# The factor of the attention scores put into the queries, and the maximum taken negated

## The chip, the cores and the metric

The kernel runs on one core of a Trainium2 chip. The metric is the device time of one execution in microseconds (us), smaller is better; a kernel's time is the median of its runs. The engines of the core work side by side, each on its own queue of instructions in a fixed order: TensorE (PE in the rows; its weight loads stand apart as PEld), VectorE (DVE), ScalarE (ACT), GpSimd (POOL), and SyncE (SP), which issues most DMAs.

## The reference

Three mixer layers run one after the other over 512 positions of width 2048: two of a first kind, which also carry 256 context positions, and one of a second kind. In a layer of the first kind the input is scaled and shifted, projected by `w_in`, and split into a short convolution, a differential attention, and a pooling part; their joined output goes through `w_out` and a layer norm. What the change touches is the differential attention. It has 8 heads, each with two maps of 64 query and key features and one value of width 128:

```python
def _diff_attn(qb, k_all, v_all, lam):
    s = jnp.einsum('bqhid,bkhid->bhiqk', qb.astype(jnp.float32) * ATTN_SCALE, k_all.astype(jnp.float32))
    p = jax.nn.softmax(s, axis=-1)
    a = p[:, :, 0] - lam * p[:, :, 1]
    return jnp.einsum('bhqk,bkhe->bqhe', a.astype(v_all.dtype), v_all)
```

`ATTN_SCALE` is 64 to the power of -0.5, 0.125. Latent queries look at 768 keys (256 of the context and 512 latent ones); in layer 0 the context's 256 queries look at the 256 context keys as well.

## The kernel before

All products are made in float32r parts: an operand is split into a high part (`hi`, a rounded copy by ScalarE) and a low part (`lo`, source minus high part, by GpSimd or VectorE), and a product is the sum of three matmuls (`mm3`, L163). A *unit* is 128 output features of the projection: 16 steps of 128 inputs, each with three matmuls over 512 latent positions and, where the context takes part, three over 256. Its weights come by DMA as raw tiles of 128x512; ScalarE copies them to `whi` (L156), GpSimd subtracts to `wlo` (L140).

`attention` (L450) runs over 8 heads, once in each of the first two layers. Per head it makes four units: queries, keys, values, gate. `evict_q` (L319) applies the rotation (L314 to L317; VectorE and GpSimd), and splits the 64 rows of each map into a high and a low half of one 128-row tile: the copies L326 and L327 on ScalarE, the subtractions L328 and L329 on VectorE (they stand under the helper's line, L140, as `Q<-qr,Q`). `evict_k` does the same with the keys, and a DMA copies the halves; `evict_v` copies the values out (L345, L346, tile `vT`), transposes and splits them.

`attend` (L361) goes over blocks of 256 queries, twice 128, and for each 128 over the two maps: matmuls give the scores in `ps_s`, of which there is one buffer (two PSUM banks); VectorE takes the maximum over a row (L384), and multiplies it by -0.125 (L386, `nb`); ScalarE takes the exponential of 0.125 times the score plus `nb`, with the row's sum (L393); VectorE takes the reciprocal of the sum (L395). After both maps it multiplies the second reciprocal by minus lambda (L398, 128x1), normalizes the first map (L400) and adds the second (L401). TensorE transposes the result (L408), which is split again (L412, L413), and multiplies it with the values (L418). A head has 6 blocks of 128 queries in layer 0 and 4 in layer 1, with two maps each: 8 x 12 + 8 x 8 = 160 passes through L384 to L395.

During attention a second job runs along (`along`, `advance`, 3 or 4 steps per unit): products of a later layer's modulation weights with a vector, GpSimd multiplying (L805) and ScalarE summing (L806) through a single buffer, with a priority moved back by 800.

The order of instructions on each engine isn't the program's: `TileContext(nc, schedule_with_timeline_sim=True)` lays it out before the run from a timeline with costs of its own, by the instructions' dependences and priorities. On the chip each engine then keeps that order, and waits on semaphores.

Of the kernel before, what the change touches and what calls it, by code (L numbers as in the profile page):

```python
# [11 lines left out]
F32 = mybir.dt.float32  # L12
F32R = mybir.dt.float32r
BF16 = mybir.dt.bfloat16
AF = mybir.ActivationFunctionType
ALU = mybir.AluOpType
AX = mybir.AxisListType
# [29 lines left out]
def mixer_stack_kernel(ctx: ExitStack, tc: tile.TileContext, a: dict, out: bass.AP):  # L47
    nc = tc.nc
# [14 lines left out]
    def ps_s():  # L63
        return pp.tile([128, 2, 512], F32, name="ps_s", tag="s", bufs=1)

    def ps_t():
        return pp.tile([128, 512], F32, name="ps_t", tag="t", bufs=1)

    def ps_v():
        return pp.tile([128, 512], F32, name="ps_v", tag="v", bufs=1)  # L70
# [68 lines left out]
    def sub_lo(lo, src, hi, eng):  # L139
        eng.tensor_tensor(lo, src, hi.bitcast(F32), op=ALU.subtract)  # L140
# [171 lines left out]
    def rope(tp, dst, ps):  # L312
        sh = tp.tile([128, NL], F32, name="rsh", tag="rsh", bufs=1)
        nc.vector.stream_shuffle(sh, ps, SWAP16)  # L314
        nc.vector.tensor_tensor(dst, ps, rope_c, op=ALU.mult)
        nc.gpsimd.tensor_tensor(sh, sh, rope_s, op=ALU.mult)
        nc.gpsimd.tensor_tensor(dst, dst, sh, op=ALU.add)  # L317

    def evict_q(ap_, aq, u, T):  # L319
        qr = aq.tile([128, NT], F32, name="qr", tag="qr", bufs=1)  # L320
        rope(aq, qr[:, :NL], u.lat)
        if u.cx is not None:
            nc.scalar.copy(qr[:, NL:], u.cx)
        Q0 = ap_.tile([128, T], F32R, name="Q0", tag="Q0", bufs=2)
        Q1 = ap_.tile([128, T], F32R, name="Q1", tag="Q1", bufs=2)
        nc.scalar.copy(Q0[0:64, :T], qr[0:64, :T])  # L326
        nc.scalar.copy(Q1[64:128, :T], qr[64:128, :T])  # L327
        sub_lo(Q0[64:128, :T], qr[0:64, :T], Q0[0:64, :T], nc.vector)  # L328
        sub_lo(Q1[0:64, :T], qr[64:128, :T], Q1[64:128, :T], nc.vector)  # L329
        return Q0, Q1  # L330

    def evict_k(ap_, aq, u):
# [28 lines left out]
    def attend(ap_, l, h, Q, K, V, SG, T):  # L361
        Q0, Q1 = Q
        Vh, Vl = V
        for qp in range(T // 256):
            nkt = 6 if qp < 2 else 2
            nk = nkt * 128
            ncol = nk // 2 if nkt == 6 else nk
            nch = nk // ncol
            aTh = ap_.tile([128, 6, 256], F32R, name="aTh", tag="aTh", bufs=1)
            aTl = ap_.tile([128, 6, 256], F32R, name="aTl", tag="aTl", bufs=1)  # L370
            for qi in range(2):
                q0 = qp * 256 + qi * 128
                es, ds = [], []
                for m, (Qm, Km) in enumerate(((Q0, K[0]), (Q1, K[1]))):
                    ps = ps_s()
                    for c in range(nch):
                        o = ps[:, c, :ncol]
                        for i, kp in enumerate(Km):
                            nc.tensor.matmul(  # L379
                                o, Qm[:, q0:q0 + 128], kp[:, c * ncol:(c + 1) * ncol], start=i == 0, stop=i == 1  # L380
                            )
                    sv = ps[:, :nch, :ncol]
                    mx = ap_.tile([128, 1], F32, name="mx", tag="mx", bufs=4)
                    nc.vector.reduce_max(mx, sv, axis=AX.XY)  # L384
                    nb = ap_.tile([128, 1], F32, name="nb", tag="nb", bufs=4)
                    nc.vector.tensor_scalar(nb, mx, -0.125, None, op0=ALU.mult)  # L386
                    if m == 0:
                        e = ap_.tile([128, NT], F32, name="E0", tag="E0", bufs=2)
                        e = e[:, :nk].rearrange("p (c n) -> p c n", c=nch)
                    else:  # L390
                        e = sv
                    d = ap_.tile([128, 1], F32, name="dn", tag="dn", bufs=4)
                    nc.scalar.activation(e, sv, AF.Exp, bias=nb, scale=0.125, accum_out=d)  # L393
                    r = ap_.tile([128, 1], F32, name="rd", tag="rd", bufs=4)
                    nc.vector.reciprocal(r, d)  # L395
                    es.append(e)
                    ds.append(r)
                nc.vector.tensor_tensor(ds[1], ds[1], neglam[l], op=ALU.mult)  # L398
                E0, E1 = es
                nc.vector.tensor_scalar(E0, E0, ds[0], None, op0=ALU.mult)  # L400
                nc.vector.scalar_tensor_tensor(E0, E1, ds[1], E0, op0=ALU.mult, op1=ALU.add)  # L401
                kt_of = lambda kt: E0[:, kt * 128 // ncol, kt * 128 % ncol:kt * 128 % ncol + 128]
                for r in range((nkt + 2) // 3):
                    n = min(3, nkt - 3 * r)
                    tp = ps_t()
                    for i in range(n):
                        kt = 3 * r + i
                        nc.tensor.transpose(tp[:, i * 128:(i + 1) * 128], kt_of(kt), ident)  # L408
                    tv = tp[:, :n * 128].rearrange("p (k d) -> p k d", k=n)
                    dh = aTh[:, 3 * r:3 * r + n, qi * 128:(qi + 1) * 128]  # L410
                    dl = aTl[:, 3 * r:3 * r + n, qi * 128:(qi + 1) * 128]
                    nc.scalar.copy(dh, tv)  # L412
                    nc.vector.tensor_tensor(dl, tv, dh.bitcast(F32), op=ALU.subtract)  # L413
            ov = ps_v()
            o = ov[:, :256]
            for kt in range(nkt):
                for p, (v, t) in enumerate(((Vh, aTh), (Vh, aTl), (Vl, aTh))):
                    nc.tensor.matmul(  # L418
                        o, v[:, kt], t[:, kt], start=(kt == 0 and p == 0), stop=(kt == nkt - 1 and p == 2)
                    )  # L420
            y = SG[:, qp * 256:(qp + 1) * 256]
            nc.vector.scalar_tensor_tensor(y, o, subg[l], y, op0=ALU.mult, op1=ALU.mult)
            o2 = ap_.tile([128, 256], F32, name="o2", tag="o2", bufs=1)
            nc.scalar.square(o2, o)
            o2h = ap_.tile([128, 256], F32R, name="o2h", tag="o2h", bufs=1)
            o2l = ap_.tile([128, 256], F32R, name="o2l", tag="o2l", bufs=1)
            nc.scalar.copy(o2h, o2)
            sub_lo(o2l, o2, o2h, nc.vector)
            msv = ps_v()
            ms = msv[:, :256]  # L430
            nc.tensor.matmul(ms, ones_r, o2h, start=True, stop=False)
            nc.tensor.matmul(ms, ones_r, o2l, start=False, stop=True)
            if qp == 0:
                rt = ap_.tile([128, 512], F32, name="rt", tag="rt", bufs=1)
                nc.scalar.copy(rt[:, :256], ms)
                continue
            r = slice(256, 512) if qp == 1 else slice(0, 256)
            nc.scalar.copy(rt[:, r], ms)
            n = 512 if qp == 1 else 256
            nc.scalar.activation(rt[:, :n], rt[:, :n], AF.Sqrt, bias=eps_t, scale=8.0)  # L440
            for i in range(n // 256):
                q0 = (0, 256)[i] if qp == 1 else 512
                ri = rt[:, i * 256:(i + 1) * 256]
                y = SG[:, q0:q0 + 256]
                nc.vector.reciprocal(ri, ri)
                nc.vector.tensor_tensor(y, y, ri, op=ALU.mult)
            o = 0 if qp == 1 else 512
            nc.sync.dma_start(Yd[4 + h][:, o:o + n], SG[:, o:o + n])
# [849 lines left out]
```

## Time and profile before

| | |
|---|---|
| median of 3 runs | 3577.58 us (3574.09 to 3579.79) |
| the profiled execution's own time | 3577.58 us |
| its span, first to last instruction | 3575.8 us |
| mean granted TensorE clock | 0.959 of full speed |
| instructions | 48562 |

Busy time adds up each engine's instructions; weight loads run beside matmuls. The idle time before an instruction is put down to the one whose semaphore came last. [...] The chain that ended last is followed back from the last instruction, at each step to what released it or to the instruction before it on its engine.

### The profile page before, as it was taken

To read this page: it belongs to the slowest core of one execution; us is meant where nothing else is said; L and a number is where in the kernel's file an instruction comes from. 1 tells how busy PE (TensorE), PEld (TensorE's weight loads), DVE (VectorE), ACT (ScalarE), POOL (GpSimd) and SP (SyncE) were. 2 spreads that over 40 slices of the span, in tenths; PEclk is the share of its full clock that TensorE was granted. 3 is DMA by queue.
4 is the path that set the end of the run, shared out by engine and by line. 5 is a ranking of instruction groups with operands and counts; after the bars stand their busy time and mean duration, and the time that the engine had idled before them with its cause. 6 is when DMAs were issued, how large, how long until landed. Compare 5 with 4: busy or idle time off the path is not lost.

```text
span 3575.8 us, 48562 instructions
## 1 busy us (share of the span) xinstructions
PE 3301.2 (92%) x16850; PEld 2791.3 (78%) x16850; DVE 2324.2 (65%) x3649; ACT 1519.0 (42%) x3181; POOL 1958.8 (55%) x1436
## 2 busy tenths in 40 slices
PE   8898998989998899999999999998989899999997
PEld 7787887878886787778888888877668777777765
DVE  6845555555468538774565555585577899996576
ACT  2255666655431222243665654322445333345333
POOL 2356776765234543256877764587776444444432
PEclk8899999989998999999999999999999999999999
DMA  8744333333246447664554542586765222223565
GB/s 311 288 133 115 99 111 99 103 104 89 70 143 185 135 131 221 191 223 140 159 154 143 162 126 85 184 309 227 231 221 195 80 93 84 84 77 109 183 222 187
DMA packets 274150, 554.72 MB, mean 155 GB/s; under 512 B 30992, under 2 KB 40048, under 8 KB 265712
## 3 DMA queue, kind: packets, MB, share of 16 engines
q1 hardware_dynamic: 271344, 539.04, 46.9%
q0 software_dynamic: 2560, 12.58, 1.8%
q8 instruction: 132, 2.16, 0.3%
q14 instruction: 114, 0.93, 0.1%
HBM read 510.69 MB, written 28.23 MB: 151 GB/s over the span
## 4 chain that ended last, share of the span: by engine, by line
PE 49%; DVE 18%; DMA 12%; issue 8%; POOL 7%; ACT 6%; SPq 0%; DVEq 0%; POOLq 0%; ACTq 0%
PE ps_m L163 35%; DVE acc L989 5%; DMA wraw<-in_w_out_dram 5%; POOL wlo L140 3%; POOL gpr L805 3%; DVE gpr L809 2%; PE ps_m L232 2%; PE ps_s L379 2%; ACT whi L156 2%; DVE wlo L140 2%; PE ps_v L418 2%; DMA gw<-in_w_ada_dram 1%; PE ps_s L233 1%; PE ps_m L609 1%; DMA gv<-in_cc_dram 1%
## 5 line engine op out<-in xcount | busy, mean ns | idle before, releaser
L163 PE MATMUL ps_m<-h,whi 128*128 128x512 f32 (+1 forms) x4736 | 1611.2, 398 | 47.3 <-ACT vT L345 32.5
L140 POOL TENSOR_TENSOR wlo<-wraw,whi 128x512 fp32r<-128x512 f32 x768 | 1113.3, 1467 | 947.6 <-ACT whi L156 886.0
L163 PEld LDWEIGHTS ps_m<-h,whi 128*128 128x128 f32 x4736 | 899.9, 192 | 233.7 <-ACT vT L345 34.1
L156 ACT CAST whi<-wraw 128x512 fp32r<-128x512 f32 x1040 | 608.1, 618 | 881.1 <-DMA wraw<-in_w_out_dram 268.0
L163 PE MATMUL ps_m<-h,wlo 128*128 128x512 f32 (+1 forms) x2368 | 940.0, 397 | 0.1
L805 POOL TENSOR_TENSOR gpr<-gw,gv 128x512 f32<-128x512 f32 x320 | 425.8, 1331 | 240.9 <-ACT gpr L806 173.1
L163 PE MATMUL ps_m<-hc,whi 128*128 128x256 f32 x2048 | 554.5, 283 | 0.0
L163 PEld LDWEIGHTS ps_m<-h,wlo 128*128 128x128 f32 x2368 | 455.1, 192 | 93.8 <-POOL wlo L140 0.8
L163 PEld LDWEIGHTS ps_m<-hc,whi 128*128 128x128 f32 x2048 | 381.0, 190 | 3.4
L140 DVE TENSOR_TENSOR wlo<-wraw,whi 128x512 fp32r<-128x512 f32 x272 | 246.7, 921 | 202.3 <-ACT whi L156 201.7
L806 ACT ACTIVATE gpr<-gpr 128x512 f32<-128x512 f32 x320 | 201.8, 631 | 233.6 <-POOL gpr L805 232.9
L163 PE MATMUL ps_m<-hc,wlo 128*128 128x256 f32 x1024 | 288.9, 282 | 0.0
L989 DVE SCALAR_TENSOR_TENSOR acc<-gu,pack,acc 128x511 f32<-128x511 f32 (+24 forms) x240 | 232.7, 981 | 5.4
L609 PE MATMUL ps_m<-wlo,y 128*128 128x512 f32 x512 | 208.1, 407 | 21.2 <-POOL wlo L140 13.6
L809 DVE SCALAR_TENSOR_TENSOR gpr<-gw,gv 128x512 f32<-128x512 f32 x232 | 220.7, 951 | 8.4 <-DMA gw<-in_w_ada_dram 2.0
L610 PE MATMUL ps_m<-whi,y 128*128 128x512 f32 x512 | 204.2, 400 | 3.2 <-DVE y L140 3.2
L384 DVE TENSOR_REDUCE mx<-ps_s 128x1 f32<-128x768 f32 (+1 forms) x160 | 135.0, 844 | 102.0 <-PE ps_s L379 101.2
L163 PEld LDWEIGHTS ps_m<-hc,wlo 128*128 128x128 f32 x1024 | 194.9, 190 | 1.0
L608 PE MATMUL ps_m<-whi,y 128*128 128x512 f32 x512 | 183.3, 400 | 1.7 <-ACT y L582 0.8
L413 DVE TENSOR_TENSOR aTl<-ps_t,aTh 128x384 fp32r<-128x384 f32 (+1 forms) x144 | 77.4, 538 | 156.2 <-ACT aTh L412 156.0
L609 PEld LDWEIGHTS ps_m<-wlo,y 128*128 128x128 f32 x512 | 98.0, 191 | 56.5 <-POOL wlo L140 22.1
L379 PE MATMUL ps_s<-K,Q 128*128 128x384 f32 x576 | 133.3, 347 | 9.5 <-ACT E L393 5.2
(353 smaller groups left out, 5284.4 us busy)
## 6 DMA issues: line engine op xcount, KB each, us to landing
wraw<-in_w_in_dram SPq DMA_DIRECT2D x640, 256.0 KB, 2.9
wraw<-in_w_out_dram SPq DMA_DIRECT2D x384, 256.0 KB, 3.5
wm<-in_w_mod_dram SPq DMA_DIRECT2D x48, 1024.0 KB, 6.9
gw<-in_w_mod_dram SPq DMA_DIRECT2D x192, 256.0 KB, 3.4
gw<-in_w_ada_dram SPq DMA_DIRECT2D x136, 256.0 KB, 3.2
wm<-in_w_ada_dram SPq DMA_DIRECT2D x14, 1024.0 KB, 6.5
K<-K POOLq DMA_DIRECT2D x32, 384.0 KB, 4.4
gv<-in_cc_dram SPq DMA_DIRECT2D x40, 256.0 KB, 3.6
```

Of the source, the lines that this page charges most:

```text
L140: eng.tensor_tensor(lo, src, hi.bitcast(F32), op=ALU.subtract)
L156: nc.scalar.copy(hi[:, sl], raw)
L163: nc.tensor.matmul(ps, w, mv[part], start=(first and p == 0), stop=(last and p == 2))
L379: nc.tensor.matmul(o, Qm[:, q0:q0 + 128], kp[:, c * ncol:(c + 1) * ncol], start=i == 0, stop=i == 1)
L384: nc.vector.reduce_max(mx, sv, axis=AX.XY)
L608: nc.tensor.matmul(ps, yh, hi[:, sl], start=(k == 0), stop=False)
L609: nc.tensor.matmul(ps, yh, lo[:, sl], start=False, stop=False)
L610: nc.tensor.matmul(ps, yl, hi[:, sl], start=False, stop=(k == KT - 1))
L805: nc.gpsimd.tensor_tensor(pr, w, t, op=ALU.mult)
L806: nc.scalar.activation(pr, pr, AF.Copy, scale=scale, accum_out=part[v][:, i:i + 1])
L809: nc.vector.scalar_tensor_tensor(junk, w, scale, t, op0=ALU.mult, op1=ALU.mult, accum_out=part[v][:, i:i + 1])
L989: nc.vector.scalar_tensor_tensor(A[:, s:], U[:, :NL - s], wj(i), A[:, s:], op0=ALU.mult, op1=ALU.add)
```

## The change

The factor 0.125 is applied when the queries are split: ScalarE's two copies become activations with a scale, VectorE's two subtractions become instructions that multiply by 0.125 and subtract. The scores then come out scaled. The maximum is taken with `negate=True`, straight into `nb`; the tile `mx` and the product by -0.125 are gone; the exponential has no scale.

```diff
         Q1 = ap_.tile([128, T], F32R, name="Q1", tag="Q1", bufs=2)
-        nc.scalar.copy(Q0[0:64, :T], qr[0:64, :T])
-        nc.scalar.copy(Q1[64:128, :T], qr[64:128, :T])
-        sub_lo(Q0[64:128, :T], qr[0:64, :T], Q0[0:64, :T], nc.vector)
-        sub_lo(Q1[0:64, :T], qr[64:128, :T], Q1[64:128, :T], nc.vector)
+        for m, Qm in enumerate((Q0, Q1)):
+            own, other = (slice(64 * i, 64 * i + 64) for i in (m, 1 - m))
+            nc.scalar.activation(Qm[own, :T], qr[own, :T], AF.Copy, scale=0.125)
+            nc.vector.scalar_tensor_tensor(
+                Qm[other, :T], qr[own, :T], 0.125, Qm[own, :T].bitcast(F32), op0=ALU.mult, op1=ALU.subtract
+            )
         return Q0, Q1
...
                     sv = ps[:, :nch, :ncol]
-                    mx = ap_.tile([128, 1], F32, name="mx", tag="mx", bufs=4)
-                    nc.vector.reduce_max(mx, sv, axis=AX.XY)
                     nb = ap_.tile([128, 1], F32, name="nb", tag="nb", bufs=4)
-                    nc.vector.tensor_scalar(nb, mx, -0.125, None, op0=ALU.mult)
+                    nc.vector.reduce_max(nb, sv, axis=AX.XY, negate=True)
...
-                    nc.scalar.activation(e, sv, AF.Exp, bias=nb, scale=0.125, accum_out=d)
+                    nc.scalar.activation(e, sv, AF.Exp, bias=nb, accum_out=d)
```

## Rows read from the trace of the kernel before

**Rows 1.** The page: busy us, share of the span, instructions of each engine.
```profile
PE 3301.2 (92%) x16850; PEld 2791.3 (78%) x16850; DVE 2324.2 (65%) x3649; ACT 1519.0 (42%) x3181; POOL 1958.8 (55%) x1436
```

**Rows 2.** Windows: busy us (instructions) of PE, PEld, DVE, ACT, POOL, PEclk, DMA share, GB/s.
```profile
240.00:1020.00 780.00, 709.41 (x4135) 627.25 (x4134) 419.42 (x753) 443.15 (x1019) 473.70 (x372) 0.95 0.34 99
1690.00:2290.00 600.00, 588.30 (x3207) 511.87 (x3206) 330.18 (x529) 336.81 (x743) 402.35 (x316) 0.99 0.47 136
...
340.50:356.50 16.00, 15.92 (x82) 14.04 (x83) 5.79 (x14) 8.19 (x22) 7.93 (x8) 0.85 0.42 110
```

**Rows 3.** TensorE's waits, 240 to 1020 us: total us, times, longest us.
```profile
PE ps_m L163 <- ACT vT L345: 32.5, 5, 8.9
PE ps_t L408 <- DVE E L401: 12.0, 3, 5.8
```

**Rows 4.** TensorE's timeline: start us, us, instruction [idle before <-releaser].
```profile
255.66 0.55 PE L353 MATMUL ps_t<-ident,vT 128*128 128x128 f32 x3 [1.38 <-ACT vT L346]
...
340.58 1.22 PE L163 MATMUL ps_m<-h,whi 128*128 128x512 f32 x2 [8.58 <-ACT vT L345]
...
916.54 1.22 PE L163 MATMUL ps_m<-h,whi 128*128 128x512 f32 x2 [3.31 <-ACT vT L345]
...
2084.68 0.97 PE L379 MATMUL ps_s<-K,Q 128*128 128x384 f32 x4 [0.57 <-DVE E L401]
```

**Rows 5.** Line 386: count, ns min/median/max, first and last start us, forms.
```profile
L386 DVE TENSOR_SCALAR nb<-mx x160: 133/153/156, 260.2 to 2250.4; 128x1 f32<-128x1 f32 x160
```

**Rows 6.** VectorE's timeline: maximum and product, the first, one other, the last.
```profile
259.17 0.96 DVE L384 TENSOR_REDUCE mx<-ps_s 128x1 f32<-128x768 f32 x1 [0.67 <-PE ps_s L379]
260.16 0.15 DVE L386 TENSOR_SCALAR nb<-mx 128x1 f32<-128x1 f32 x1
...
1894.14 0.94 DVE L384 TENSOR_REDUCE mx<-ps_s 128x1 f32<-128x768 f32 x1
...
1898.97 0.15 DVE L386 TENSOR_SCALAR nb<-mx 128x1 f32<-128x1 f32 x1
...
2249.36 0.96 DVE L384 TENSOR_REDUCE mx<-ps_s 128x1 f32<-128x768 f32 x1 [0.91 <-PE ps_s L379]
2250.36 0.15 DVE L386 TENSOR_SCALAR nb<-mx 128x1 f32<-128x1 f32 x1
```

**Rows 7.** The chain that ended last, 240 to 2290 us: start us, us, piece.
```profile
351.50 0.17 DVE nb L386
...
2070.37 0.16 DVE nb L386
```

**Rows 8.** Lines of the split and like them: count, ns min/median/max, starts, forms.
```profile
L326 ACT CAST Q<-qr x16: 610/722/836, 244.1 to 2155.9; 64x768 fp32r<-64x768 f32 x8, 64x512 fp32r<-64x512 f32 x8
L140 DVE TENSOR_TENSOR Q<-qr,Q x32: 685/966/2061, 245.1 to 2157.3; 64x768 fp32r<-64x768 f32 x16, 64x512 fp32r<-64x512 f32 x16
L156 ACT CAST whi<-wraw x1040: 601/620/652, 19.6 to 3550.2; 128x512 fp32r<-128x512 f32 x174
L806 ACT ACTIVATE gpr<-gpr x320: 612/632/650, 249.1 to 2111.3; 128x512 f32<-128x512 f32 x160
L737 ACT ACTIVATE h<-xT,s x16: 706/722/727, 15.9 to 123.2; 128x512 fp32r<-128x512 f32 x16
L140 DVE TENSOR_TENSOR wlo<-wraw,whi x272: 624/693/1834, 1302.9 to 3550.8; 128x512 fp32r<-128x512 f32 x136
L793 DVE SCALAR_TENSOR_TENSOR gv<-gw,gv x40: 681/693/1827, 347.9 to 2010.0; 128x512 f32<-128x512 f32 x40
```

**Rows 9.** Lines 398 and 400: count, ns min/median/max, first and last start us, forms.
```profile
L398 DVE TENSOR_TENSOR rd<-rd,neglam x80: 147/161/7137, 269.3 to 2251.8; 128x1 f32<-128x1 f32 x80
L400 DVE TENSOR_SCALAR E<-E,rd x80: 353/678/4321, 261.7 to 2244.8; 128x768 f32<-128x768 f32 x64, 128x256 f32<-128x256 f32 x16
```

**Rows 10.** Groups of instructions: count | busy us, mean ns | idle us before.
```profile
L398 DVE TENSOR_TENSOR rd<-rd,neglam 128x1 f32<-128x1 f32 x80 | 41.1, 514 | 2.5
```

**Rows 11.** The chain that ended last, around 1901 us.
```profile
1901.00 7.15 DVE rd L398
```

## The prediction

> **What bounds the kernel now.** I read five views, from the whole to the one instruction. First the busy shares of the page: TensorE is busy for 92% of the span, VectorE for 65%, ScalarE for 42%, GpSimd for 55% [rows 1]. So only what lets TensorE run without idling, or at a higher clock, can move the end. Second, the windows of the two attention stages, the only code that the diff touches: 240 to 1020 us (layer 0) and 1690 to 2290 us (layer 1) [rows 2]. TensorE is busy for 709.4 of 780 us in the first and 588.3 of 600 us in the second; the idle time is 70.6 and 11.7 us, 82.3 us together. VectorE is busy for 419 of 780 and 330 of 600 us, a little over half: it bounds nothing by its sum. [...]
>
> Third, whom TensorE waited for in the first stage: the eviction of the values (vT, ScalarE), 32.5 us in 5 waits, then the mixed probabilities E (VectorE), 12.0 us in 3 [rows 3]. These are ends of a head: the last block of scores, the table loads for square root and exponential and the evictions of the next head stand in ScalarE's and VectorE's queues together. Fourth, TensorE's timeline has 30 idle times over 0.3 us (23 and 7; the first and the last, and the first and the last of the nine over 3 us in layer 0, in [rows 4]). The nine last 52.0 us, 5.8 on average. A long one costs twice: in the 16 us after the gap that ends at 340.58 the granted clock is 0.85 [rows 2], which is 16 x 0.15 = 2.4 us more. Fifth, the chain that ended last, for how often the instruction that the change removes lies on it.
>
> **The change, part by part.** *The small product.* For each of 160 score blocks (16 heads' blocks of 128 queries, two maps each) VectorE now runs the maximum, then the product nb. It takes 153 ns at the median, between 133 and 156 [rows 5], so 160 x 0.15 = 24 us of VectorE's time go. From the end of the maximum to the end of nb it is 259.17 + 0.96 = 260.13 to 260.16 + 0.15 = 260.31, 0.18 us; I use 0.19 with the rounding [rows 6]. That is the usual delay, but nb often stands behind other work on VectorE: in the middle pair the maximum ends at 1895.08 and nb at 1899.12, 4.04 us later [rows 6]. Counted along VectorE's timeline (160 pairs, first and last in [rows 6]), 64 have another instruction between, and all delays together make 99 us. With the maximum itself as the bias, ScalarE's exponential may start that much earlier.
>
> Little of it lies on the path. On the chain nb has eleven pieces in the two stages, of 0.17 us at the most (first and last in [rows 7]): 11 x 0.19 = 2.1 us at most, counting the handing on. The rest lies beside TensorE's projections, which run through while a score block is on its way. That cover is gone at the 30 idle times: if each of them became shorter by one delay, 30 x 0.19 = 5.7 us. Lower end 0, because in place of nb another wait may end as late. I take 3.4 us, between the count on the chain and the count of the idle times. What is late next is the exponential itself, then the reciprocal behind it.
>
> *The negated maximum.* No row shows one. Its bounds are 0 more than the plain maximum and a second pass as long as nb, 0.15 us [rows 5], which would undo the whole part; I take 0, since nothing more is read or written. [...]
>
> *The exponential without its factor* has the same shape and the same operands; its factor is an immediate now, as in the multiply by a constant of L806, and I take 0. If the immediate cost anything it would be the 12 ns of the next part, 160 x 0.012 = 1.9 us of ScalarE's time, a gain, beside TensorE's work.
>
> *The split of the queries.* Per head two copies on ScalarE become multiplications by 0.125, and two subtractions on VectorE become multiply-and-subtract; 32 of each. A copy of 64x512 takes 610 ns at the least, of 64x768 836 at the most [rows 8]. The nearest rows: for 128x512, the copy L156 takes 620 ns, the multiplication by an immediate L806 632, that by a column of factors L737 722 [rows 8]. So 12 to 102 ns more, 32 x that is 0.4 to 3.3 us; I take 0.4, since the factor is an immediate. On VectorE the subtraction of 128x512 takes 624 at the least and 693 at the median, the three-operand form with an immediate (L793) 681 and 693: 0 to 57 ns more, 32 x that is 0 to 1.8 us; I take 0.9. No queue is passed and no wait is added; behind the split on VectorE stand the key's split and the maxima, behind them TensorE's next unit. The cover is again the projections of the head. If it were gone everywhere, the loss would be 3.3 + 1.8 = 5.1 us; with a quarter of 1.3 on the path, 0.3.
>
> The sum is -3.4 + 0.3 = -3.1 us. The profiled execution took 3577.58 us (span 3575.8 and 1.8 around it), and that is also the median of the three runs. So 3577.58 - 3.1 = 3574.5 us.
>
> **A second-order effect** belongs to every case: the order of instructions on each engine is laid out by the planner from its own timeline, and 160 instructions fewer shift it. I see no sign for it in the profile; it widens the bounds of all cases.
>
> **The rivals.** *Gaps close.* The exponentials that nb delays by more than its own 0.19 us hold up what stands behind them in ScalarE's queue, among it the copies for the weights and the sums of GpSimd's products. Freed, the end of a head could come without TensorE running dry. For it: 64 delays of that kind, and nine long gaps. Against it: the gaps' last waits are on vT, five times, not on nb [rows 3]. Each closed gap gives 5.8 + 2.4 = 8.2 us; with two of nine, 16.4, and with the 3.1 of the forecast -19.5: 3558 us.
>
> *More collisions with GpSimd (slower).* The tiny product of the reciprocal with lambda (L398) takes 161 ns at the median, but up to 7137 [rows 9]; the 80 take 41.1 us [rows 10], which is 41.1 - 80 x 0.161 = 28.2 us more than they need. The normalization L400 shows the same, 353 to 4321 ns [rows 9]. The worst L398 starts at 1901.00 and is on the chain for its full 7.15 us [rows 11]; the sum L401 and TensorE's transpositions stand behind it. nb itself is never held up so. If the scores arrive earlier, these two may fall into GpSimd's trains more often. For it: one stall of this size outweighs the whole gain. Against it: they may as well fall out of the trains. Half as much again of L398's 28.2 us would be +14.1, less 3.1: 3588.6 us. It is a loss from 3.1 us of added stalls on the path, one by 0.2% from about 10.3. [...]
>
> *The change does not do what it says:* the negation costs a second pass, so nothing is saved, and the split is dearer by its upper bounds on a path share of a quarter, 5.1 / 4 = 1.3 us: 3578.9 us.
>
> **How the numbers follow.** The forecast, 3574.5 with a range of its own from 3569 to 3580 (the bounds -5.7 and +1.3, and some shift by the planner), has a chance of 0.44; gaps close 0.29; more collisions 0.20; nothing saved 0.07. A measurement of this kernel can tell about 0.2% from no change, 7.2 us: the bounds are 3570.4 and 3584.7. Faster takes the 0.29 and 0.07 from the lower edge of the forecast, 0.36. Slower takes the 0.20. Within 0.2% is 0.37 + 0.07 = 0.44. The range reaches to the middle of the two big cases on each side, from 3557 to 3590: it leaves out a little under half of the gaps' case and nearly half of the collisions'.
>
> **What would show it.** After the change there is no nb row; ScalarE's exponential names the maximum as its releaser; 160 maxima at 0.95 us for 128x768, or 1.1 if the negation is a pass of its own. VectorE's time in the two stages falls by about 24 us. TensorE's idle time there falls from 82 us to about 79. The forecast is wrong if the idle time goes below 70 or the mean clock of layer 0 rises above 0.96 (gaps close), or if L398 takes more than 51 us in all, 10 more than its 41.1 (collisions).

## The result, and the profile after

The changed kernel takes 3558.36 us (median of 6 runs, 3556.84 to 3568.92) against 3579.18 us for the kernel before in the same series. The ratio is 0.9946 [0.9932, 0.996]. It is faster by 0.54%, some 19 us (the two medians differ by 20.8), where 3.1 us were forecast. Its profiled execution took 3560.77 us. All line numbers below are those of the kernel that is named. In the changed kernel the scores are L381, the maximum is L386 and goes straight into `nb`, the exponential is L393, and L398, L400 and L401 are as before.

The page of the changed kernel, against [rows 1]:
```profile
span 3559.0 us, 48355 instructions
...
PE 3295.3 (93%) x16850; PEld 2782.2 (78%) x16850; DVE 2289.7 (64%) x3489; ACT 1518.4 (43%) x3181; POOL 1956.4 (55%) x1436
```
VectorE has 160 instructions and 34.5 us less. 24 us are the product's; the diff takes nothing else away that would account for the other 10. The span fell by 16.8 us (3575.8 to 3559.0). TensorE's idle time, the span less its busy time, has 10.9 of them (274.6 to 263.7 us).

The windows of the two attention stages, against [rows 2], with the same columns:
```profile
240.00:1020.00 780.00, 708.31 (x4137) 624.26 (x4136) 411.63 (x668) 448.19 (x1027) 474.77 (x371) 0.96 0.34 99
1690.00:2290.00 600.00, 591.69 (x3217) 513.20 (x3215) 323.80 (x479) 337.13 (x741) 400.43 (x312) 1.00 0.48 142
```
TensorE idles 71.7 and 8.3 us, 80.0 together, where it was 82.3. Such windows mislead a little: work has moved across their edges, so a stretch that became shorter is filled with the next one's work. From here on stretches are cut by work: at the issue on SyncE of a given load of raw weights (`wraw`, L155, counted from 0). Such a cut is fair only where TensorE has the same matmuls in it, or nearly so. Between loads 44 and 192 (layer 0's attention and the steps behind it), before and after:
```profile
262.94:1141.82 878.88, 790.76 (x4558) 696.71 (x4557) 515.75 (x950) 458.64 (x1043) 508.83 (x391) 0.94 0.38 110
259.70:1127.88 868.18, 788.98 (x4572) 693.48 (x4571) 490.28 (x835) 459.98 (x1043) 509.96 (x393) 0.96 0.37 111
```
and between loads 384 and 512 (layer 1's attention and the steps behind it), before and after:
```profile
1727.24:2274.28 547.04, 535.34 (x2938) 466.79 (x2937) 306.38 (x491) 308.23 (x682) 363.55 (x286) 0.99 0.46 133
1714.27:2258.20 543.93, 535.62 (x2938) 465.66 (x2937) 289.51 (x430) 306.43 (x681) 364.29 (x286) 1.00 0.47 134
```
Of the 16.8 us the first has 10.7 and the second 3.1. These are single executions, and the executions of the kernel before lie between 3574.09 and 3585.8 us, so a difference of a few us in one stretch says little by itself.

The groups that the diff touches, and the two that collide with GpSimd (columns: line, engine, operation, count | busy us, mean ns | idle us before). Two of the kernel before:
```profile
L384 DVE TENSOR_REDUCE mx<-ps_s 128x1 f32<-128x768 f32 (+1 forms) x160 | 135.0, 844 | 102.0 <-PE ps_s L379 101.2
L400 DVE TENSOR_SCALAR E<-E,rd 128x768 f32<-128x768 f32 (+1 forms) x80 | 83.3, 1041 | 2.7
```
The changed kernel:
```profile
L386 DVE TENSOR_REDUCE nb<-ps_s 128x1 f32<-128x768 f32 (+1 forms) x160 | 135.2, 845 | 114.5 <-PE ps_s L381 113.3
L400 DVE TENSOR_SCALAR E<-E,rd 128x768 f32<-128x768 f32 (+1 forms) x80 | 71.0, 887 | 2.6
...
L329 DVE SCALAR_TENSOR_TENSOR Q<-qr,Q 64x768 fp32r<-64x768 f32 (+1 forms) x32 | 39.0, 1219 | 11.0 <-ACT Q L328 10.2
L398 DVE TENSOR_TENSOR rd<-rd,neglam 128x1 f32<-128x1 f32 x80 | 34.9, 436 | 2.5
...
L328 ACT ACTIVATE Q<-qr 64x768 fp32r<-64x768 f32 (+1 forms) x32 | 23.5, 736 | 10.1 <-POOL qr L317 9.6
```
The maximum took 844 ns before and takes 845 negated. The copies of the split took 724 ns on average and take 736 with the factor. The product with lambda, L398, fell from 41.1 us [rows 10] to 34.9, and the normalization L400 from 83.3 to 71.0. The change edits neither.

What TensorE waited for in layer 0's stage, against [rows 3]:
```profile
PE ps_m L163 <- ACT vT L347: 35.1, 7, 7.8
PE ps_t L408 <- DVE aTl L413: 13.2, 6, 5.7
...
PE ps_t L408 <- DVE E L401: 1.5, 2, 1.3
```
The ends of the heads still wait for vT (32.5 us before). The gap of 8.58 us at 340.58 [rows 4] is 0.30 us now, at 332.14, and others have grown: in this window the places of the gaps are new, not their sum.

In layer 1 the place that matters is the head whose product with lambda took 7.14 us before [rows 11]. VectorE's timeline of the changed kernel there:
```profile
1880.13 0.16 DVE L395 RECIPROCAL rd<-dn 128x1 f32<-128x1 f32 x1 [0.16 <-ACT ps_s L393]
1880.33 0.82 DVE L398 TENSOR_TENSOR rd<-rd,neglam 128x1 f32<-128x1 f32 x1
1881.18 1.02 DVE L401 SCALAR_TENSOR_TENSOR E<-ps_s,rd,E 128x768 f32<-128x768 f32 x1
```

### The profile page after: what moved, and what is told of

Its sections match the earlier page's. It is cut to its first block, busy times and chain, and to the rows that moved or that the text cites. A ratio compares the mean times of both kernels' runs of the same rounds, so it can differ in the third digit from the quotient of the medians.

```text
span 3559.0 us, 48355 instructions
## 1 busy us (share of the span) xinstructions
PE 3295.3 (93%) x16850; PEld 2782.2 (78%) x16850; DVE 2289.7 (64%) x3489; ACT 1518.4 (43%) x3181; POOL 1956.4 (55%) x1436
## 5 line engine op out<-in xcount | busy, mean ns | idle before, releaser
L163 PE MATMUL ps_m<-h,whi 128*128 128x512 f32 (+1 forms) x4736 | 1614.8, 398 | 50.2 <-ACT vT L347 35.1
L140 DVE TENSOR_TENSOR wlo<-wraw,whi 128x512 fp32r<-128x512 f32 x272 | 239.2, 893 | 202.9 <-ACT whi L156 202.6
L609 PE MATMUL ps_m<-wlo,y 128*128 128x512 f32 x512 | 205.5, 402 | 18.1 <-POOL wlo L140 10.9
L386 DVE TENSOR_REDUCE nb<-ps_s 128x1 f32<-128x768 f32 (+1 forms) x160 | 135.2, 845 | 114.5 <-PE ps_s L381 113.3
L282 DVE SCALAR_TENSOR_TENSOR wm<-wm,ca 128x2048 f32<-128x2048 f32 x50 | 128.8, 2575 | 21.0 <-DMA wm<-in_w_ada_dram 11.6
L381 PE MATMUL ps_s<-K,Q 128*128 128x384 f32 x576 | 133.9, 346 | 8.3 <-ACT E L393 6.6
```

What stands on the lines that cost most here:

```text
L163: nc.tensor.matmul(ps, w, mv[part], start=(first and p == 0), stop=(last and p == 2))
L381: nc.tensor.matmul(o, Qm[:, q0:q0 + 128], kp[:, c * ncol:(c + 1) * ncol], start=i == 0, stop=i == 1)
L386: nc.vector.reduce_max(nb, sv, axis=AX.XY, negate=True)
L609: nc.tensor.matmul(ps, yh, lo[:, sl], start=False, stop=False)
```

## The experiments

Taking 160 instructions away gave the planner another timeline and so another order: in the traces, 12361 of TensorE's 16850 matmuls have the same tiles and shape at the same place before and after. So the diff changes two things, the work and the order, and the experiments hold one and vary the other. The kernel builds itself twice. A first build of the work `PLAN` is laid out freely, and its order is read. A second build, of the work `WORK`, is held to that order by edges that add no semaphore; a product that only one of the two has stands behind its maximum. The traces show the order held: all 16850 matmuls of experiment 1 stand, by tiles and shape, as in the kernel before, and those of experiments 2 and 4 as in the changed kernel.

```diff
+    order = None if PLAN is None else _order(*_emit(arrays, PLAN))
+    nc, _ = _emit(arrays, WORK, order)
...
+                for x, y in zip(want, want[1:]):
+                    tc.add_manual_dep(made[y], made[x].name, nosync, reason="order of the other plan")
```

In these dictionaries `scaled` is the factor in the split, and `product` the small product behind the maximum (0, 1 or 2 of them). The median of the kernel before was 3577.49 us beside experiments 1 to 4, 3576.2 beside 5 to 8, 3575.46 beside 9 and 10, and 3579.95 beside 11 and 12.

**1. The new work in the old order.**
```diff
+WORK = {"scaled": True, "product": False}
+PLAN = {"scaled": False, "product": True}
```


> The changed kernel's work (scaled split, negated maximum, no product nb), but on every engine the instructions are kept in the order that the kernel before has, with nb left out. Theory 'order': the gain of 0.54% comes from the new layout that the planner makes, so here only the shorter step remains: 2 to 6 us under before, ratio 0.9985 to 0.9995. Rival 'direct': the freed exponentials close the gaps, so nearly the whole gain stays: ratio 0.995 to 0.996.

Measured: 3570.66 us (12 runs), ratio 0.9987 [0.9976, 0.9997]. The work alone gives 0.13%, 4.6 us (the medians differ by 6.8). In its profile the stretch between loads 44 and 192 takes 867.12 us.

**2. The old work in the new order.**
```diff
+WORK = {"scaled": False, "product": True}
+PLAN = {"scaled": True, "product": False}
```


> The work of before (copies and subtractions for the split, product nb by -0.125), but every engine's instructions stand in the changed kernel's order, with each nb right behind its maximum on VectorE. Theory 'order': most of the gain is here, 13 to 16 us, ratio 0.9955 to 0.9965. Rival 'direct': no gain, ratio 0.999 to 1.001. If both this and the run in the old order show a part, the two parts should add up to the 0.9946 measured for the whole change.

Measured: 3567.25 us (9 runs), ratio 0.9973 [0.9963, 0.9983]. A kernel that does all the old work, the 160 products too, gains twice as much from the order alone; the intervals of the two parts, 0.03 to 0.24% and 0.17 to 0.37%, still overlap. Its groups, the columns as above:
```profile
L411 DVE TENSOR_SCALAR E<-E,rd 128x768 f32<-128x768 f32 (+1 forms) x80 | 70.9, 886 | 2.6
L409 DVE TENSOR_TENSOR rd<-rd,neglam 128x1 f32<-128x1 f32 x80 | 34.5, 431 | 2.5
L394 DVE TENSOR_SCALAR nb<-mx 128x1 f32<-128x1 f32 x160 | 24.6, 154 | 5.5
```
nb is there with its 24.6 us, and still the two colliding groups have the changed kernel's low times (105.4 us together, 105.9 in the changed kernel, 124.4 before). They go with the order, not with the work: in the first experiment, with the old order, they took 44.0 and 86.4.

**3. The split alone, in the old order.**
```diff
+WORK = {"scaled": True, "product": True}
+PLAN = {"scaled": False, "product": True}
```


> Only the split: queries scaled by ScalarE and VectorE, the maximum plain, nb kept as a product by -1.0, the exponential without scale, in the order of before. Every theory here expects little: by the prediction's rows 0.3 us more, at most 5 us; ratio 0.9995 to 1.0015. If the scaled copy were much dearer than a plain one, 32 x 0.1 us would show in the split's rows as 0.72 us in place of 0.62 for 64x512.

Measured: 3578.18 us (12 runs), ratio 1.0001 [0.999, 1.0012]. The split costs and gives nothing that shows.

**4. The changed kernel with its own order held**, the control for the method.
```diff
+WORK = {"scaled": True, "product": False}
+PLAN = {"scaled": True, "product": False}
```


> The changed kernel with its own order held by the same means as in the crossed runs: nothing differs from the changed kernel. Both theories expect its ratio of 0.9946, within 0.9932 to 0.9960; another value would mean that holding an order costs or gains something by itself.

Measured: 3563.66 us (10 runs), ratio 0.9959 [0.9944, 0.9975]. The two parts add up: -0.13% and -0.27% make -0.40%, measured -0.41%. The changed kernel itself, 0.9946 [0.9932, 0.996], lies a little lower; the intervals overlap.

**5. The new work in an order planned with two products behind each maximum.**
```diff
+WORK = {"scaled": True, "product": False}
+PLAN = {"scaled": True, "product": 2}
```


> The changed kernel's work in an order that the planner makes for two products behind each maximum; neither product is in the kernel. Theory 'less to plan is better': the order gets worse with the planned products, so this is no faster than the order of before (one product, 0.9987), ratio 0.9985 to 1.002. Rival 'each order is a new draw': anything from 0.993 to 1.002, without regard to the count.

Measured: 3626.09 us (4 runs), ratio 1.0135 [1.0111, 1.016]. The very instructions of the changed kernel, in another order, take 50 us more than the kernel before. Its profile, of the slowest of the four runs, puts +18.4 us between loads 44 and 192 and +25 between 384 and 512 against the kernel before. In layer 1 one product with lambda again takes far over its usual 0.16 us (it is held), at another place. VectorE's timeline there:
```profile
1783.14 6.53 DVE L416 TENSOR_TENSOR rd<-rd,neglam 128x1 f32<-128x1 f32 x1
1789.70 1.02 DVE L419 SCALAR_TENSOR_TENSOR E<-ps_s,rd,E 128x768 f32<-128x768 f32 x1
```
and TensorE's first instruction behind it:
```profile
1790.87 0.88 PE L426 MATMUL ps_t<-ident,E 128*128 128x128 f32 x3 [3.38 <-DVE E L419]
```

**6 and 7. The new work in orders planned with the product for one of the two maps only**, the second (6) or the first (7).
```diff
-PLAN = {"scaled": True, "product": 2}
+PLAN = {"scaled": True, "product": {(0, 1): 1, (1, 1): 1}}
...
+PLAN = {"scaled": True, "product": {(0, 0): 1, (1, 0): 1}}
```


> The changed kernel's work in an order planned with the product for the second map of each head alone (80 of 160). Theory 'less to plan is better': between the order without products (0.9946 and 0.9959 measured) and that with 160 (0.9987), near 0.997. Rival 'new draw': as likely outside that stretch, above 0.9995 or below 0.994, as inside.

> The same with the product planned for the first map alone (80 of 160). 'Less to plan is better' gives near 0.997 here and the same as for the second map; 'new draw' lets the two halves differ by more than their intervals.

Measured: 3571.99 us, 0.9986 [0.9974, 0.9999] for the second map, and 3579.95 us, 1.0008 [0.9994, 1.0021] for the first (12 runs each). Half of the products in the plan does not give half of the gain, and the first half is no better than the kernel before: the gain does not go with their number. Each plan looks like a throw of its own, and what it is worth has to be found in the place where it differs. In the profile of 6 three products with lambda are held in layer 1 (5.47, 6.49 and 5.44 us), and the stretch from load 384 to load 512 takes 555.7 us, where experiments 1 and 8 take 551.6 and 551.0. In that of 7 the loss is in layer 0: 887.0 us between loads 44 and 192, against 865.5 to 872.2 in experiments 1, 4, 8 and 9 and the changed kernel, with no product over 1.77 us there. So an order can cost as much in layer 0 by other waits, which were not followed.

**8 and 9. The new work in orders planned with the product in one layer only**, layer 1 (8) or layer 0 (9); the other layer then stands as in the changed kernel.
```diff
+PLAN = {"scaled": True, "product": {(1, 0): 1, (1, 1): 1}}
...
+PLAN = {"scaled": True, "product": {(0, 0): 1, (0, 1): 1}}
```


> The changed kernel's work; the order is planned with the products in layer 1 alone, which gives the changed kernel's order up to the end of layer 0's attention and nearly that of before from layer 1's on. If the order's gain comes from layer 0 (gaps at the ends of heads and in the first convolution and pooling steps behind it, which the stages of the crossed runs suggest: some 9 us), 0.996 to 0.9968; if from layer 1, 0.998 to 0.9992.

> The work of the changed kernel (no small product anywhere), in an order planned with the small product in layer 0's attention only: layer 0 stands near the order of the kernel before, layer 1 is planned as in the changed kernel. It is the complement of the run before it, in which only layer 1 was planned with the product (0.9977 [0.9964, 0.999], between the two values it was to tell apart). Theory 1 (the order's gain sits in layer 1's attention, where the stretch between the 384th and the 448th weight load lasted 297.1 and 298.9 us in the two runs with the old order and 288.5 and 290.9 us in the two with the new one): 0.996, some 3563 us. Theory 2 (it sits in layer 0's attention): 0.9987, some 3571 us. Theory 3 (both carry a part and the parts add): 0.997, some 3566 us. A time outside 0.9955 to 0.9995 would say that a plan changed in one layer is a draw of its own for the other too.

Measured: 3566.52 us, 0.9977 [0.9964, 0.999] with the old order in layer 1 (11 runs), and 3561.86 us, 0.996 [0.9946, 0.9974] with the old order in layer 0 (6 runs). The first alone was inconclusive, since it lies between its two expected values. The second settles most of it: with layer 0 in the old order nothing that can be told of the gain is lost (0.996 against 0.9959 in experiment 4), so most of what these two orders differ by sits in layer 1. The profiles agree in direction. Between loads 384 and 448 the two kernels with the new work and layer 1's old order took 298.9 and 297.1 us (experiments 1 and 8); the three with its new order took 290.9, 288.5 and 291.5 (4, the changed kernel, 9). Part of these 8 us is work that the new order puts behind load 448: TensorE has 1583 and 1580 matmuls in the stretch in the old order, 1568 or 1569 in the new. To load 512 the counts agree; experiments 1 and 4, in the columns of [rows 2]:
```profile
1711.57:2263.21 551.64, 539.05 (x2938) 469.28 (x2937) 303.74 (x431) 307.91 (x682) 360.46 (x286) 0.99 0.47 132
1707.58:2254.56 546.98, 535.92 (x2938) 465.59 (x2937) 288.74 (x430) 306.43 (x681) 363.22 (x286) 1.00 0.47 133
```
With 551.0 in experiment 8, 546.4 in 9 and 543.9 in the changed kernel, layer 1's new order is worth some 5 us there. With the old work it does not show (547.0 in the kernel before and 550.6 in experiment 3, 547.5 in 2). Between loads 44 and 192 the means differ by 2 us (869.6 for 1 and 9, 867.5 for the others).

**10. One move in the new order: the vT copies early.** Since gaps of 35 us end with vT, ScalarE's two copies were put directly behind the second copy of K in layer 0's heads, ahead of the last exponential.
```diff
+    for h in range(8):
+        for n, name in enumerate(work["vt"][2 * h:2 * h + 2]):
...
+            q.insert(q.index(keys[work["k"][2 * h + 1]]) + 1 + n, keys[name])
```


> The changed kernel's own order, held, with one move on ScalarE: in each of layer 0's eight heads the two vT copies (for whose PSUM TensorE waits) stand directly behind the second K copy, ahead of the last exponential, the casts and the sums of the side work. No work is left out. Theory (what stands on ScalarE ahead of the vT copies sets the long idle times at the heads' ends): in the changed kernel six of them, 34.9 us together, end with vT; 1.3 to 4.7 us of other ScalarE work stand between the second K copy and vT, of which VectorE's part of the K split (about 1.2 us, vT takes the buffer it reads) has to be waited for in any case, so each shrinks by 0 to 3 us, some 8 us together, of which up to half comes back behind them: 3555 to 3560 us, ratio 0.993 to 0.995, and the vT idle times sum to 25 to 28 us. Rival (the exponential that now stands behind the copies and their wait is late instead, and TensorE waits for E or for the side work): the vT idle times shrink and others grow by as much: 0.9955 to 0.9985, 3563 to 3572 us.

Measured: 3579.66 us (11 runs), 1.0008 [0.9996, 1.002]: all of the gain is lost, 0.49% against experiment 4, so the theory fell. TensorE's waits in the same window as above:
```profile
PE ps_m L163 <- ACT vT L352: 31.5, 6, 7.8
...
PE ps_v L430 <- ACT aTh L424: 10.7, 6, 3.3
```
The vT waits shrank by 3.6 us, and the waits for the probabilities' split, `aTh`, rose from 1.2 to 10.7 us. The reason stands in the two queues at one head's end, ScalarE's
```profile
517.04 0.83 ACT L345 CAST K<-qr 64x768 fp32r<-64x768 f32 x1
521.44 0.86 ACT L352 COPY vT<-ps_m 128x512 f32<-128x512 f32 x2 [3.57 <-DVE K L140]
```
and VectorE's:
```profile
517.05 3.37 DVE L457 RECIPROCAL rt<-rt 128x256 f32<-128x256 f32 x2 [2.05 <-ACT rt L452]
520.45 0.96 DVE L140 TENSOR_TENSOR K<-qr,K 64x768 fp32r<-64x768 f32 x1
```
vT takes the buffer that VectorE's split of K still reads, and that split stands behind 3.37 us of reciprocals. What stood ahead of vT on ScalarE had been cover. With vT first, ScalarE waits 3.57 us, and the exponential waits behind it. This is one head's end; the whole stretch between loads 44 and 192 takes 887.0 us against 865.5 in experiment 4, TensorE's idle time has 14 us of the difference, and not all of it was followed.

**11 and 12. The product with lambda with one tensor less**, in the old order (11) and in the new one (12). The kernel leaves out lambda's value, in all 80 products of both layers.
```diff
-                nc.vector.tensor_tensor(ds[1], ds[1], neglam[l], op=ALU.mult)
+                nc.vector.tensor_scalar(ds[1], ds[1], -0.5, None, op0=ALU.mult)
```


> The changed kernel's work in the order of the kernel before (the same instructions at the same places as in the first experiment), with one operand less: the product of the second map's reciprocal with lambda (tile rd, 80 instructions of one column) multiplies by the number -0.5 in place of the tile neglam, so that it reads one tensor where it read two. What it leaves out is lambda's value. Theory (the order's gain in layer 1 is this product waiting for GpSimd: in the four runs with layer 1's old order it once takes 7.13 to 7.18 us beside an unbroken run of GpSimd instructions, in the four with the new one never over 1.33 us; products with a number, the 160 of tile nb, never took over 0.156 us): no such instruction is over 0.2 us, their sum falls from 44 to about 12.5 us, layer 1's stretch between the 384th and the 448th weight load goes from 298.9 to 290 to 293 us, and the ratio from 0.9987 to 0.995 to 0.997 (3559 to 3567 us). Rival 1 (an instruction with one tensor is held as well, or the E product behind it takes over the wait: that one also reached 7.96 us): the sum or that of the E products stays, and so does the time, 0.998 to 0.9995. Rival 2 (the holding goes, but TensorE's time does not hang on it): the sum falls and the ratio stays at 0.998 to 0.9995.

> The same edit (the number -0.5 in place of the tile neglam, lambda's value left out) in the changed kernel's own order, held: the counterpart of the fourth experiment (0.9959 [0.9944, 0.9975]). Theory: here no product of tile rd takes over 1.8 us, so that only their sum falls, from 34.7 to about 12.5 us of VectorE time, on whose chain few of them stand: 0.9945 to 0.9962 (3557 to 3563 us), and the difference to the run before it, 0.9 to 1 us in 1000 or less, says that the holding was most of what the two orders differed by. Rival 1 (the new order gains by other things): this run stays 0.002 or more below the run before it. Rival 2 (the time goes with VectorE's busy time wherever it is): 0.993 to 0.994.

Measured: 3561.29 us, 0.9953 [0.9936, 0.997] (6 runs) in the old order, and 3563.0 us, 0.9954 [0.9935, 0.9973] (7 runs) in the new one. Without the second tensor no difference of the two orders shows. The edit gives 0.34% in the old order (0.9987 before it) and nothing that can be told in the new (0.9959). So the old order loses time by these products, and of the new one no such loss shows; the intervals, some 0.2% on each difference, are too wide for a finer sum.

The place itself, in experiment 1. VectorE's timeline:
```profile
1890.11 0.16 DVE L406 RECIPROCAL rd<-dn 128x1 f32<-128x1 f32 x1 [1.86 <-ACT ps_s L404]
1890.31 7.13 DVE L409 TENSOR_TENSOR rd<-rd,neglam 128x1 f32<-128x1 f32 x1
1897.48 1.02 DVE L412 SCALAR_TENSOR_TENSOR E<-ps_s,rd,E 128x768 f32<-128x768 f32 x1
```
GpSimd's beside it:
```profile
1889.95 2.55 POOL L140 TENSOR_TENSOR wlo<-wraw,whi 128x512 fp32r<-128x512 f32 x2
1892.46 1.29 POOL L816 TENSOR_TENSOR gpr<-gw,gv 128x512 f32<-128x512 f32 x1
1893.71 2.49 POOL L140 TENSOR_TENSOR wlo<-wraw,whi 128x512 fp32r<-128x512 f32 x2
1896.17 1.25 POOL L816 TENSOR_TENSOR gpr<-gw,gv 128x512 f32<-128x512 f32 x1
```
and TensorE's next instruction that needs the result:
```profile
1898.64 0.87 PE L419 MATMUL ps_t<-ident,E 128*128 128x128 f32 x3 [3.96 <-DVE E L412]
```
GpSimd runs from 1889.95 to 1897.42 without a break, through six instructions, and the product of one column ends with it, at 1897.44. So it is everywhere: all 13 products with lambda over 1.9 us in the kept traces (kernel before and experiments 1, 3, 5, 6, 7 and 8) end 0.02 to 0.03 us after an unbroken run of GpSimd. The same place in experiment 11, VectorE's timeline:
```profile
1886.87 0.16 DVE L406 RECIPROCAL rd<-dn 128x1 f32<-128x1 f32 x1 [1.86 <-ACT ps_s L404]
1887.07 0.15 DVE L410 TENSOR_SCALAR rd<-rd 128x1 f32<-128x1 f32 x1
1887.26 1.02 DVE L415 SCALAR_TENSOR_TENSOR E<-ps_s,rd,E 128x768 f32<-128x768 f32 x1
```
with the same six instructions of GpSimd around it:
```profile
1886.86 2.56 POOL L140 TENSOR_TENSOR wlo<-wraw,whi 128x512 fp32r<-128x512 f32 x2
1889.39 1.29 POOL L819 TENSOR_TENSOR gpr<-gw,gv 128x512 f32<-128x512 f32 x1
1890.65 2.53 POOL L140 TENSOR_TENSOR wlo<-wraw,whi 128x512 fp32r<-128x512 f32 x2
1893.15 1.28 POOL L819 TENSOR_TENSOR gpr<-gw,gv 128x512 f32<-128x512 f32 x1
```
and TensorE's transposition without a gap ahead of it:
```profile
1891.27 0.49 PE L422 MATMUL ps_t<-ident,E 128*128 128x128 f32 x3
```
GpSimd's run is as long, the product takes 0.15 us, and TensorE's gap ahead of the transposition is gone. The stretch from load 384 to load 448, in the columns of [rows 2], for experiment 1
```profile
1711.57:2010.45 298.88, 288.03 (x1583) 251.50 (x1582) 177.30 (x233) 180.17 (x414) 221.19 (x176) 0.98 0.54 151
```
and for experiment 11:
```profile
1712.91:2001.66 288.75, 283.85 (x1589) 247.67 (x1588) 157.04 (x233) 179.53 (x414) 223.37 (x176) 1.00 0.56 156
```
10.1 us less, 9.0 to load 512 (551.6 to 542.7). VectorE, with 233 instructions in both, is busy for 20.3 us less, TensorE's idle time goes from 10.9 to 4.9, and the granted clock from 0.98 to 1.00 of full speed. The median of all runs says 9.4 us (3570.66 to 3561.29; by the ratios 0.34%, 12 us). The spans of these two profiled executions differ by 3.4 us only (3563.4 and 3560.0); over all other stretches together experiment 11 is the slower, by 6.7 us. Two holdings account for it: besides the one shown, another of 4.84 us at 1812.48. The kernel before has both (7.14 and 4.80), and so have experiments 3 and 8; the kernels with the new order have no product over 1.33 us in that stretch. They do not keep all of the 9 us: TensorE waits there 6.7 us for the first map's exponential in experiment 4 and 4.9 in the changed kernel, which it does not in experiment 1.

## Why the prediction was right and wrong

The time lies in the range, at its low edge, but not at the forecast, nor in the forecast's own range from 3569 to 3580. That the range holds it is luck: its lower end, 3557, was set by the case of closing gaps. The forecast was the work's share; the larger share came from a step that the prediction left at nothing.

- **The small product.** Gain taken as 3.4 us; the work as a whole was forecast at -3.1. Experiment 1 measures the work at -0.13%, 4.6 us, with an interval from 1.1 to 8.6. Right as far as the interval can tell.
- **The negated maximum.** Taken as free: 845 against 844 ns, x160. Right.
- **The split.** Taken as 12 ns more per copy on ScalarE: 736 against 724. On VectorE 0 to 57 ns more were allowed: 39.0 us for 32 against 38.5, 17 ns each; in experiment 3 they took 37.7. On the path 0.3 us were taken; experiment 3 measures 1.0001 [0.999, 1.0012]. Right.
- **TensorE's idle time in the stages.** Forecast 79 us, measured 80.0, and neither of the two tests fired that were to show the forecast wrong: idle time under 70 us or a clock of layer 0 over 0.96, and L398 over 51 us. The forecast was wrong all the same. The fixed windows hide it: the stretches became shorter, by 10.7 us between loads 44 and 192, with 8.9 us less of TensorE's idle time (88.1 to 79.2), and by 3.1 between 384 and 512.
- **The planner's order: the failed step.** The prediction called it second-order, saw "no sign for it in the profile", and let it widen the bounds only. It is -0.27% [-0.37, -0.17] (experiment 2), about 10 us, against 0.13% for the work. With the new work, experiments 9 and 11 place most of it: two products with lambda that GpSimd held in layer 1's attention come, in the new order, at moments when GpSimd does not hold them for long (no product over 1.33 us in that stretch). The holdings cost some 9 us there (experiment 11), of which the new order keeps some 5 in the profiles; the rest of its 10 us has no place that the traces would show beyond their scatter.
- **The sign was there.** [Rows 9 to 11] show one product of one column at 7137 ns, on the chain that ended last for its full length. That it is GpSimd that holds it stands in none of these rows and was the author's reading; the timelines of the kernel before bear it out, with six instructions of GpSimd without a break from 1900.64 to 1908.11 us and the product from 1901.00 to 1908.14. The prediction used these rows for the rival on the slow side alone (more collisions, L398 over 51 us) and granted in half a sentence that they "may as well fall out of the trains". That is the side that came: L398 fell to 34.9 us. Whether it was the likelier one is not shown; in the three other fresh orders of both layers (experiments 5, 6 and 7) the 80 products took 43.3, 50.6 and 42.4 us, more than the 41.1 of the kernel before. Priced as in the rows, the 7.0 us over its usual 0.16 of the worst case on the chain would have given the forecast under half of the 16 us that it missed.
- **Gaps close** named 3558 us, which is the measured number, by two of the nine long gaps, of which the longest wait for vT. That did not happen: the vT waits went from 32.5 to 35.1 us. The new order closes some gaps of layer 0 and opens others, and by experiment 9 layer 0's new order is worth nothing that can be told against the old one. On a smaller scale waits did close, with the new work alone too. TensorE's waits in layer 0 of the kernel before, from the view of [rows 3], have two put down to the small product:
```profile
PE ps_m L163 <- DVE nb L386: 4.1, 1, 4.1
PE ps_t L408 <- DVE nb L386: 2.0, 1, 2.0
```
With the new work in layer 0's old order they are gone, TensorE idles 82.7 and 84.2 us between loads 44 and 192 (experiments 1 and 9; 88.1 before), and the stretch takes 867.1 and 872.2 us (878.9 before, 879.0 in experiment 3). The profiles thus give the work up to 12 us in layer 0; the runs of experiment 1 bound the whole of it at 8.6.

What stays open: how the gain divides between work and order within the intervals; why the order in experiment 7 costs layer 0 some 15 us or more; experiment 8 left 0.1% of gain, within the intervals, to layer 0's order; the changed kernel is 0.13% faster than its own held order, also within them. Of the 50 us that experiment 5 loses only the 6.53 us in layer 1 were followed to their cause.

## What to carry to other kernels

Where a planner lays out the instructions, an edit that removes or adds any is two edits: hold the old order with the new work, and the new order with the old work, before crediting either. When the chain that ended last has one instruction at forty times its usual length, price its disappearance as well as its return: any reordering throws that die again, and the surer gain is a form of the instruction that was never seen held (here a number in place of the second tensor, 156 ns at the most in all 80 cases of experiment 11). When a stretch is cut at a load, count the matmuls in it before comparing two orders. Before pulling a copy forward in a queue, look at what it will wait for there; the work that it overtakes may have been its cover.

## What the runs showed of the hardware

- A VectorE product of two 128x1 tensors took 7.13 to 7.18 us at one place of four of these kernels, and ended with GpSimd's run of six instructions beside it, 0.02 to 0.03 us after the run's last. So one hold can last over several of GpSimd's instructions. The same product with a number in place of the second tensor took 141 to 156 ns in all 80 cases of experiment 11, one of them beside the same run. By what the run holds the form with two tensors, and not the one with a number, no run shows. In experiment 5 the held product is recorded from 1783.14 us, 0.25 us ahead of GpSimd's run.
- The normalization by a column of factors (L414 in experiment 11) still took up to 4345 ns, 774 at the median, so the long cases were not all taken away; those that remained made no difference that could be told between the two orders.
- One set of instructions took between 0.9946 and 1.0135 of the time of the kernel before, by its order alone (the changed kernel and experiment 5).
